# A Mamba-2 and latent-attention inference step on one core: a new step table for the scan's seven steady groups and the output projection

## The chip, the core and the metric

The kernel runs on one core of a Trainium2 chip. The metric is device time in microseconds, the median of several executions. The core has TensorE (PE in the profile; its weight loads are PEld), VectorE (DVE), ScalarE (ACT), GpSimd (POOL) and SyncE (SP, which here only issues DMAs), each with a queue of its own that it works through in order.

## What is computed

Layer 0 is a Mamba-2 state-space layer, layer 1 a latent attention; both see a prompt of 1024 rows and 8 samples of 8 rows, 1088 rows in all, with D = 1024. What the change touches is layer 0 from the input projection to the output projection, cut here to its core:

```python
def ssd_mixer(h, conv_buf, ssm_state, w_in, conv_w, conv_b, dt_bias, a_log, d_skip, norm_w, w_out):
    proj = jnp.einsum('btd,de->bte', h, w_in)
    z, xbc, dt_raw = ...                       # 2048, 2048 + 2*8*128, 32 columns
    xbc, new_buf = causal_conv(xbc, conv_buf, conv_w, conv_b)
    xbc = jax.nn.silu(xbc.astype(F32))         # xs: 32 heads x 64; bm, cm: 8 groups x 128
    y, new_state = ssd_scan(xs, dt, a_head, bm, cm, ssm_state.astype(F32))
    y = y + d_skip.astype(F32)[:, None] * xs
    y = y.reshape(b, t, SSD_D_INNER) * jax.nn.silu(z.astype(F32))
    yg = y.reshape(b, t, SSD_GROUPS, SSD_D_INNER // SSD_GROUPS)
    yg = yg * lax.rsqrt(jnp.mean(yg * yg, axis=-1, keepdims=True) + NORM_EPS)
    out = jnp.einsum('bte,ed->btd', yg.reshape(b, t, SSD_D_INNER) * norm_w, w_out)
```

In ssd_scan a chunk of 128 rows needs, for each of a group's four heads, the decay matrix exp(segment sums) masked to its lower triangle and multiplied with C B^T, that product times x*dt, and a state that goes from chunk to chunk.

## The kernel before

All matmuls work on split numbers: a float32 operand is kept as a high part (a cast to fp32r, on ACT, L129) and a low part (the difference, on DVE or POOL, L130), and a product is three matmuls, high by high, high by low and low by high. So "part p is split" means a cast and a subtraction behind it, of 512 columns of weights, from a raw buffer that a DMA filled ("wraw", two buffers) into "wih" and "wil" (five buffers each). A raw buffer is free for the next load when the low half is done.

The layer runs over 8 groups of heads. ssd_groups treats groups 1 to 7 in the same way, in 21 steps each (t = 0 to 20). In a step of group g TensorE computes one 24-matmul piece of g's input projection (Flow.proj): for t below 12 a block of 128 columns (x, B and C channels, four blocks) for one of three groups of tokens, from t = 12 on the z gate. The other engines meanwhile do the convolution of g (Flow.ew) and the scan of the group before (Scan.ew, Scan.pe), which has 8 chunks of the prompt and a ninth, of 64 rows, for the samples. Behind group 7 a loop of the same form goes through the last scan and through the output projection: OutProj "a" takes the first eight 128-row blocks of w_out, OutProj "b" the other eight, each 18 pieces, one a step, started at steps A0 = 9 and B0 = 27. Its PSUM results are poa and pob. WOut brings w_out's blocks, 512 KB each, and splits them with norm_w (hi on ACT L1053, lo on DVE L1054).

The order of each engine's queue is the order of the program's text (a manual schedule): one step is `ev = fl.proj(t)`, `scan.ew(t)`, `fl.ew(t)`, `ev()` (the eviction of the piece's PSUM on ACT, L571 to L586), `scan.pe(t)`, `fl.pe(t)`. What an instruction waits for is set by tiles and their buffers. PSUM has two banks "tr" (transposes, among them trp, ctp and s0p), two "pj" (projection), and one each for cb, y, pv and st.

Chunk i of the scan: front(i) at step 2i-2 transposes x and B into trp and computes cb = C B^T; front1(i) at step 2i-1 (for i = 0 at step 0) reads these from PSUM: xsT (ACT L699), xdt (DVE L701), BTh and BTl, xdd (POOL), cbm = cb times the mask (DVE L708), and takes four Relu on M (ACT L710). M is the chunk's matrix of summed logarithms, loaded from DRAM by SP (L672, 256 KB), issued a step or two before. front2(i) at step 2i takes Exp of M (L719) and multiplies it with cbm (L723); decayed splits xdd into xddh and xddl, state updates S (L757), out1 and out2 make y. front(i+1) writes the one cb bank, so it waits for cbm of chunk i. From t = 12 on the samples' states come in four parts: turn_state transposes a part into s0p (L826), split_state makes sh and sl of it, state_rows multiplies (pv, L847), add_state and stores follow. copies, turn_copies, triples and blocks prepare the sample rows (b3, xf, x3, bb) for that, in two halves.

In Flow.ew there stand also: the splits of the weights, two per block one step apart (and load(p+2) behind each), parts 10 and 11 both at t = 11; the Silu of the convolved channels at t = 16 and 17 (L626, L627), that of z at 18; the copy "co" of the last three rows of each sequence's channels out of PSUM (ctp, L631) at t = 14 and their six DMAs at t = 15. OutProj scales y by a group's 1/rms, yrs: a pow on POOL over [128, 9x4] (L204, rstd_of), once for a and once for b.

## Time and profile before

| what | us |
|---|---|
| median of 3 runs | 2189.02 |
| lowest and highest run | 2186.99, 2199.06 |
| the profiled execution | 2191.87 |
| its span, first to last instruction | 2190.1 |
| groups 2 to 7, each (five of the windows) | 112.6 to 112.8 |
| output stage before its projection / from poa's first to pob's first matmul | 50.5 / 135.1 |
| the core's mean granted TensorE clock | 0.941 |

Times in the profile's rows are microseconds from the span's start. A window gives the busy time of each engine in a stretch; in the list of waits, a row names the engine and line that waited, the engine and line it waited for, and the total, the number of times and the longest. A timeline row has start, duration, engine, line, operation, output<-input, and in brackets the idle time before it with what ended it.

### The profile page before, as it was taken

How to read it: one execution, taken by the hardware profiler on the slowest of the kernel's cores; microseconds unless marked ns; L12 is line 12 of the kernel's file. 1: busy time of each engine (PE TensorE's matmuls, PEld its weight loads, DVE VectorE, ACT ScalarE, POOL GpSimd, SP SyncE). 2: the span in 40 equal slices, each digit the busy share in tenths (PEclk: the TensorE clock that was granted, in tenths of full speed). 3: DMA queues.
4: the chain of work that ended last, by engine and by line, in shares of the span. 5: the costliest groups of instructions: out<-in, count | busy, mean ns of one | idle time of the engine just before them, and what ended most of it. 6: DMA issues, size and time to landing. Idle time of an engine off the chain costs nothing.

```text
span 2190.1 us, 33508 instructions
## 1 busy us (share of the span) xinstructions
PE 1983.4 (91%) x12001; PEld 1805.7 (82%) x12001; DVE 1245.8 (57%) x2558; ACT 1089.8 (50%) x2547; POOL 809.8 (37%) x977
## 2 busy tenths in 40 slices
PE   6969999999998989858999899979999999989998
PEld 5968988888898989747788799868888887768887
DVE  4427474646465655555443522446787878776665
ACT  5345555555555556553211422433676766655553
POOL 1226364546464646463200001201333333665551
PEclk9979999999899989859999999989999989989999
DMA  4012232323232222244554433132111111364541
GB/s 138 19 54 85 71 88 69 91 59 89 72 85 76 83 73 78 77 146 133 156 179 154 160 140 99 49 99 100 42 43 43 41 41 45 107 211 145 147 135 50
DMA packets 186478, 206.55 MB, mean 94 GB/s; under 512 B 23132, under 2 KB 151912, under 8 KB 185928
## 3 DMA queue, kind: packets, MB, share of 16 engines
q1 hardware_dynamic: 181480, 185.40, 28.1%
q0 software_dynamic: 4752, 18.88, 2.7%
q8 instruction: 95, 1.56, 0.3%
q14 instruction: 71, 0.58, 0.1%
q10 hardware_dynamic: 80, 0.13, 0.0%
HBM read 151.05 MB, written 53.28 MB: 93 GB/s over the span
## 4 chain that ended last, share of the span: by engine, by line
PE 57%; DVE 17%; ACT 8%; issue 7%; DMA 5%; POOL 4%; SPq 1%; POOLq 0%; ACTq 0%; DVEq 0%
PE pj L88 16%; PE pq L100 5%; PE pj L100 5%; PE poa L100 5%; PE pob L100 4%; PE py L734 2%; DVE acc L617 1%; DVE tl L1632 1%; PE pk L100 1%; PE pz L100 1%; POOL kvl L1913 1%; DVE sc L1591 1%; DVE wil L130 1%; PE p L100 1%; PE vp L88 1%
## 5 line engine op out<-in xcount | busy, mean ns | idle before, releaser
L88 PE MATMUL pj<-xh,wih 128*128 128x384 f32 (+1 forms) x768 | 255.8, 337 | 18.0 <-ACT wih L129 9.3
L88 PE MATMUL pj<-xh,wil 128*128 128x384 f32 (+1 forms) x768 | 254.5, 332 | 2.7 <-DVE wil L130 2.0
L88 PE MATMUL pj<-xl,wih 128*128 128x384 f32 (+1 forms) x768 | 254.7, 332 | 0.0
L100 PE MATMUL pj<-wih,xh 128*128 128x256 f32 x504 | 158.9, 319 | 13.5 <-ACT wih L129 13.5
L100 PE MATMUL pj<-wil,xh 128*128 128x256 f32 (+1 forms) x504 | 155.1, 314 | 11.8 <-DVE wil L130 11.8
L88 PEld LDWEIGHTS pj<-xh,wih 128*128 128x128 f32 x768 | 145.9, 191 | 20.0 <-ACT wih L129 9.6
L617 DVE SCALAR_TENSOR_TENSOR acc<-raw,vec,acc 128x1112 f32<-128x1112 f32 x84 | 134.8, 1605 | 40.0 <-ACT acc L613 40.0
L1632 POOL TENSOR_TENSOR tl<-P,th 128x384 fp32r<-128x384 f32 (+1 forms) x96 | 89.6, 933 | 181.9 <-ACT P L1630 137.4
L88 PEld LDWEIGHTS pj<-xh,wil 128*128 128x128 f32 x768 | 146.0, 190 | 7.4 <-DVE wil L130 7.4
L88 PEld LDWEIGHTS pj<-xl,wih 128*128 128x128 f32 x768 | 146.4, 191 | 0.3
L100 PE MATMUL pj<-wih,xl 128*128 128x256 f32 x448 | 139.7, 312 | 0.0
L1629 ACT ACTIVATE th<-st 128x512 fp32r<-128x512 f32 x192 | 94.4, 492 | 74.8 <-PE st L1625 56.2
L100 PEld LDWEIGHTS pj<-wih,xh 128*128 128x128 f32 x504 | 110.8, 220 | 14.9 <-ACT wih L129 14.9
L100 PEld LDWEIGHTS pj<-wil,xh 128*128 128x128 f32 (+1 forms) x504 | 107.8, 214 | 15.3 <-DVE wil L130 14.7
L771 POOL TENSOR_TENSOR y<-y,xD 128x256 f32<-128x256 f32 x64 | 82.1, 1284 | 102.5 <-DVE y L770 102.2
L723 DVE TENSOR_TENSOR M<-M,cbm 128x512 f32<-128x512 f32 (+1 forms) x72 | 54.3, 755 | 91.7 <-ACT M L719 91.7
L1913 POOL TENSOR_TENSOR kvl<-pgr,kvh 128x1024 fp32r<-128x1024 f32 x32 | 78.2, 2445 | 73.4 <-ACT kvh L1912 73.4
L100 PEld LDWEIGHTS pj<-wih,xl 128*128 128x128 f32 x448 | 100.2, 224 | 0.0
L130 POOL TENSOR_TENSOR xddl<-xdd,xddh 128x256 fp32r<-128x256 f32 x64 | 69.2, 1081 | 83.3 <-ACT xddh L129 82.6
L130 DVE TENSOR_TENSOR wil<-wraw,wih 128x512 fp32r<-128x512 f32 x88 | 65.0, 740 | 58.4 <-ACT wih L129 57.5
L710 ACT ACTIVATE M<-M,tok 128x128 f32<-128x128 f32 (+1 forms) x288 | 90.5, 388 | 12.6 <-DMA M<-acs_d 12.5
L1630 ACT ACTIVATE P<-st 128x512 f32<-128x512 f32 x192 | 93.4, 486 | 0.0
(1001 smaller groups left out, 6393.1 us busy)
## 6 DMA issues: line engine op xcount, KB each, us to landing
wraw<-in_ssd_w_in SPq DMA_DIRECT2D x92, 256.0 KB
M<-acs_d SPq DMA_DIRECT2D x64, 256.0 KB
y_d<-xD SPq DMA_DIRECT2D x64, 128.0 KB
s<-in_state_ssm SPq DMA_DIRECT2D x32, 256.0 KB
out_s_ssm<-s SPq DMA_DIRECT2D x32, 256.0 KB
wraw<-in_ssd_w_out SPq DMA_DIRECT2D x16, 512.0 KB
q_d<-qt SPq DMA_DIRECT2D x32, 192.0 KB
qp<-q_d SPq DMA_DIRECT2D x8, 768.0 KB
```

The lines of the kernel that those rows point to most:

```text
L88: nc.tensor.matmul(out, a, b, start=(i == 0), stop=(i == n - 1))
L100: nc.tensor.matmul(o, a, b, start=(j == 0), stop=(j == len(ops) - 1))
L130: (eng or nc.vector).tensor_tensor(lo, src, hi.bitcast(F32), op=ALU.subtract)
L617: nc.vector.scalar_tensor_tensor(acc, raw[:, j : j + n], k.convw[j][:, blk : blk + 1], acc, op0=ALU.mult, op1=ALU.add)
L710: nc.scalar.activation(M[:m, h, :m], M[:m, h, :m], AF.Relu, bias=c.tk[:, 0, 4 * g + h : 4 * g + h + 1], scale=-1.0)
L723: nc.vector.tensor_tensor(M[:m, :, :m], M[:m, :, :m], c.cbm[:m, :m].unsqueeze(1).to_broadcast([m, 4, m]), op=ALU.mult)
L734: nc.tensor.matmul(py[:m, h * 64 : h * 64 + 64], c.M[:m, h, :m], c.xdt[:m, h * 64 : h * 64 + 64], start=True, stop=True)
L771: nc.gpsimd.tensor_tensor(y[:m], y[:m], c.xD[:m], op=ALU.add)
L1629: nc.scalar.activation(th[:, :n], ps[:, :n], AF.Exp, scale=SCALE)
L1630: nc.scalar.activation(P[:, :n], ps[:, :n], AF.Exp, scale=SCALE)
L1632: eng.tensor_tensor(tl[:, :n], P[:, :n], th[:, :n].bitcast(F32), op=ALU.subtract)
L1913: nc.gpsimd.tensor_tensor(rl, raw, rh.bitcast(F32), op=ALU.subtract)
```

## The change

The pieces of the step are put in another order, and some into another step.

- A new method weights_in, called right behind the projection's matmuls and ahead of the scan's work, splits parts 2 to 10 of the weights one step sooner than before, part 11 stays at t = 11 behind the scan's and Flow's work. The next group's part 0 is loaded at t = 10 (was 11) and split at t = 18 (was 19).
- The Silu of x, B, C and of the first z half move into after(t), behind the step's eviction. The copy co moves from t = 14 to 17, its DMAs from 15 to 18, the transposes into ctp from 13 to 16.
- front1 takes the four Relu on M first, then ACT's two PSUM readings (xsT, BTh), then DVE's (xdt, BTl, cbm). front2 comes ahead of decayed; xD goes into a method skip behind out1; add_state goes to the step's end. The second half of the copies moves from t = 14 to 12 and its transposes from 15 to 13; third (b3, xf) is at 11 and 14, triples (bb, x3) at 12 and 16.
- w_out's blocks 0 to 3 are loaded in step 18 of group 7, into four raw buffers; ACT's halves of blocks 0 to 8 are made at steps 0 to 5 ahead of the scan's work, DVE's behind it. Blocks 9 to 15 are loaded from step 21 on through two raw buffers (10 and 11 used to be loaded at steps 9 and 10) and split at steps 21 to 24. A0 becomes 7, B0 25. The pow for a is taken tile by tile ([128, 4]) at t below 9 of group 7, that for b at step 22.

On ScalarE at the start of group 5 (the scan of group 4: xsT4_0 is chunk 0's x, M4_0 its matrix, raw50 the first evicted piece, wih_6577 weights of group 5) stood

```order
L699 COPY xsT4_0_6515<-trp4_0_6474 128x256
L129 CAST BTh4_0_6519<-trp4_0_6474 128x128
L710 ACTIVATE M4_0_6472<-M4_0_6472,tok_71 128x128 x4
L129 CAST xddh4_0_6531<-xdd4_0_6523 128x256
L719 ACT_TABLE_LOAD
L719 ACTIVATE M4_0_6472<-M4_0_6472 128x512
L571 COPY raw50_6481<-pj5_0_6480 128x384
L699 COPY xsT4_1_6572<-trp4_1_6540 128x256
```

and stands now

```order
L700 ACTIVATE M4_0_6472<-M4_0_6472,tok_71 128x128 x4
L702 COPY xsT4_0_6525<-trp4_0_6474 128x256
L705 CAST BTh4_0_6527<-trp4_0_6474 128x128
L722 ACT_TABLE_LOAD
L722 ACTIVATE M4_0_6472<-M4_0_6472 128x512
L129 CAST xddh4_0_6539<-xdd4_0_6533 128x256
L571 COPY raw50_6481<-pj5_0_6480 128x384
L129 CAST wih_6577<-wraw_6468 128x512
```

The four Relu, which read what M's DMA brings, went from behind the two PSUM readings to ahead of them, in chunk 0 as in chunk 1.

On ScalarE in steps 10 and 11 of group 4 (wih is a part of the weights, raw43 an evicted piece, M3_6 the matrix of chunk 6; the first list begins with part 9 and ends with parts 10 and 11, the second begins with part 10 and ends with part 11) stood

```order
L129 CAST wih_5840<-wraw_5702 128x512
L571 COPY raw43_5714<-pj4_10_5794 128x384
L699 COPY xsT3_6_5888<-trp3_6_5849 128x256
L129 CAST BTh3_6_5892<-trp3_6_5849 128x128
L710 ACTIVATE M3_6_5821<-M3_6_5821,tok_71 128x128 x4
L129 CAST Ch3_6_5904<-acc30_4035 128x128
L779 ACTIVATE y3_4_5836,yssq_70<-xD3_4_5691 128x256
L799 CAST b33False_5911<-x3p3False_5855 96x128
L806 CAST x33False_5916<-xf3False_5914 96x256
L129 CAST wih_5919<-wraw_5773 128x512
L129 CAST wih_5926<-wraw_5844 128x512
```

and stands now

```order
L129 CAST wih_5825<-wraw_5689 128x512
L722 ACTIVATE M3_5_5691<-M3_5_5691 128x512
L129 CAST xddh3_5_5837<-xdd3_5_5766 128x256
L129 CAST Sh3_4_5842<-S3_5_5752 128x256
L571 COPY raw43_5720<-pj4_10_5800 128x384
L700 ACTIVATE M3_6_5833<-M3_6_5833,tok_71 128x128 x4
L702 COPY xsT3_6_5898<-trp3_6_5855 128x256
L705 CAST BTh3_6_5900<-trp3_6_5855 128x128
L129 CAST Ch3_6_5910<-acc30_4041 128x128
L786 ACTIVATE y3_4_5846,yssq_70<-xD3_4_5708 128x256
L806 CAST b33False_5917<-x3p3False_5861 96x128
L129 CAST wih_5923<-wraw_5750 128x512
```

Part 10 went to step 10, into the place of part 9 and ahead of chunk 5's Exp; part 11 is where it was, behind the Relu of chunk 6 and what follows them.

On SyncE in steps 10 to 11 of group 4 the queue was

```order
L541 DMA wraw_5773<-in_ssd_w_in 128x2x256
L821 DMA s030_5819<-in_state_ssm 128x4x128
L672 DMA M3_6_5821<-acs_d_1074 128x512
L541 DMA wraw_5844<-in_ssd_w_in 128x2x256
L821 DMA s031_5884<-in_state_ssm 128x4x128
L780 DMA y_d_82<-xD3_4_5691 128x256
```

and is now

```order
L541 DMA wraw_5829<-in_ssd_w_in 128x4x128
L830 DMA s030_5831<-in_state_ssm 128x4x128
L673 DMA M3_6_5833<-acs_d_1074 128x512
L830 DMA s031_5890<-in_state_ssm 128x4x128
L787 DMA y_d_82<-xD3_4_5708 128x256
L541 DMA wraw_5927<-in_ssd_w_in 128x4x128
```

The load ahead of s030 and M3_6 brought part 10 of group 4 (two blocks of 256 columns); now it brings part 0 of group 5 (four of 128), into a raw buffer that part 10 of group 4 has to leave first.

The diff, cut to its core:

```diff
+    def weights_in(self, t):
+        if t < 9 and t % 3 < 2:
+            p = 2 * (t // 3) + 2 + t % 3
+        elif 8 <= t < 11:
+            p = t
+        else:
+            return
+        self.split(p)
+        if p < 10:
+            self.load(p + 2)
+
     def ew(self, t):
         k, g, nc = self.k, self.g, self.k.nc
-        if t < 9 and t % 3:
-            p = 2 * (t // 3) + 1 + t % 3
-            self.split(p)
-            self.load(p + 2)
-        if t in (9, 10):
-            self.split(t - 1)
-            self.load(t + 1)
-        if t == 11:
-            self.split(10)
...
+        if t == 17:
+            self.co = self.rp.tile([128, RAW], F32, tag="raw", name=f"co{g}", bufs=2)[:27, :512]
+            nc.vector.tensor_copy(self.co, self.ctp[:27])
+        if t == 18:
...
+    def after(self, t):
+        nc = self.k.nc
         if t in (16, 17):
             acc, xs = self.xc[t - 16]
             nc.scalar.activation(acc[:, :, :SEQ], acc[:, :, :SEQ], AF.Silu)
             nc.scalar.activation(xs.rearrange("p a (b w) -> p a b w", w=NT),
                                  bass_window(acc, SEQ + 3, NT + 3, NT), AF.Silu)
-        if t == 14:
...
-        if t == 15:
...
         if t == 18:
             nc.scalar.activation(self.z[0], self.z[0], AF.Silu)
-    def late(self, t):
-        if t == 11:
-            self.split(11)
 
     def pe(self, t):
-        if t == 13:
+        if t == 16:
...
         smp = i == 8
+        for h in range(4):
+            nc.scalar.activation(M[:m, h, :m], M[:m, h, :m], AF.Relu, bias=c.tk[:, 0, 4 * g + h : 4 * g + h + 1], scale=-1.0)
         xsT = c.xsT = self.tile([128, 256], "xsT", "xsT" + tag, 1)
         nc.scalar.copy(xsT[:m], p[:m, 0:256])
+        if not smp:
+            c.Bh, c.Bl = (self.tile([128, 128], "BT" + x, "BT" + x + tag, 2, F32R) for x in "hl")
+            nc.scalar.copy(c.Bh, p[:, 256:384])
         xdt = c.xdt = self.tile([128, 256], "xdt", "xdt" + tag, 2)
         nc.vector.tensor_tensor(c.v3(xdt), c.v3(p[:, 0:256]), c.hb(1), op=ALU.mult)
         if not smp:
-            c.Bh, c.Bl = (self.tile([128, 128], "BT" + x, "BT" + x + tag, 2, F32R) for x in "hl")
-            split(k, c.Bh, c.Bl, p[:, 256:384])
+            nc.vector.tensor_tensor(c.Bl, p[:, 256:384], c.Bh.bitcast(F32), op=ALU.subtract)
             c.xdd = self.tile([128, 256], "xdd", "xdd" + tag, 1)
             nc.gpsimd.tensor_tensor(c.v3(c.xdd), c.v3(xsT), c.hb(2), op=ALU.mult)
         cbm = c.cbm = self.tile([128, 128], "cbm", "cbm" + tag, 1)
         nc.vector.tensor_tensor(cbm[:m, :m], c.cb[:m, :m], (k.masks if smp else k.masku)[:m, :m], op=ALU.mult)
-        for h in range(4):
-            nc.scalar.activation(M[:m, h, :m], M[:m, h, :m], AF.Relu, bias=c.tk[:, 0, 4 * g + h : 4 * g + h + 1], scale=-1.0)
...
         nc.scalar.activation(M[:m, :, :m], M[:m, :, :m], AF.Exp, scale=-1.0)
-        c.xD = self.tile([128, 256], "xD", "xD" + c.tag, 2)
-        nc.gpsimd.tensor_tensor(c.v3(c.xD), c.v3(c.xsT), k.dsk[:m, self.hs].unsqueeze(2).to_broadcast([m, 4, 64]),
-                                op=ALU.mult)
         nc.vector.tensor_tensor(M[:m, :, :m], M[:m, :, :m],
                                 c.cbm[:m, :m].unsqueeze(1).to_broadcast([m, 4, m]), op=ALU.mult)
+
+    def skip(self, i):
+        k, c = self.k, self.c[i]
+        m = c.m
+        c.xD = self.tile([128, 256], "xD", "xD" + c.tag, 2)
+        k.nc.gpsimd.tensor_tensor(c.v3(c.xD), c.v3(c.xsT), k.dsk[:m, self.hs].unsqueeze(2).to_broadcast([m, 4, 64]),
+                                  op=ALU.mult)
...
-            if t in (14, 16, 18, 20):
-                self.add_state((t - 14) // 2)
             if i == 0:
                 self.front1(0)
+            if i <= 8:
+                self.front2(i)
             if i < 8:
                 self.decayed(i)
             if 1 <= i <= 8:
                 self.state(i - 1)
-            if i <= 8:
-                self.front2(i)
-            if 1 <= i <= 8:
                 c = self.c[i - 1]
                 self.out1(c, c.py, c.py[:, 256:] if i > 1 else None)
+            if i <= 8:
+                self.skip(i)
+            if t in (14, 16, 18, 20):
+                self.add_state((t - 14) // 2)
         else:
             if t in (13, 15, 17, 19):
                 self.split_state((t - 13) // 2)
...
                 self.front1(i + 1)
             if 1 <= i <= 8:
                 self.out2(self.c[i - 1])
-        if t in (9, 14):
-            self.copies(t == 14)
-        if t in (11, 16):
+        if t in (9, 12):
+            self.copies(t == 12)
+        if t in (11, 14):
+            self.third(t == 14)
+        if t in (12, 16):
             self.triples(t == 16)
-        if t in (12, 16):
-            self.blocks(t == 16)
...
-        if t in (10, 15):
-            self.turn_copies(t == 15)
+        if t in (10, 13):
+            self.turn_copies(t == 13)
...
-        rstd_of(k, self.rs, k.yssq[:, :, k0 // 2 : k0 // 2 + self.ng], 256)
+        self.rs = k.rs
...
-    def split(self, kk, pool=None):
+    def split(self, kk, pool):
         nc, raw = self.k.nc, self.raw.pop(kk)
-        hi, lo = ((pool or self.pool).tile([128, D], F32R, name=f"wo{x}{kk}") for x in "hl")
...
+        nc.scalar.activation(hi, raw, AF.Copy, scale=self.k.ssdn[:, kk : kk + 1])
+        self.late.append((raw, hi, lo, kk))
         return hi, lo
+
+    def low(self):
+        for raw, hi, lo, kk in self.late:
+            self.k.nc.vector.scalar_tensor_tensor(lo, raw, self.k.ssdn[:, kk : kk + 1], hi.bitcast(F32),
+                                                  op0=ALU.mult, op1=ALU.subtract)
+        self.late = []
...
-A0, B0 = 9, 27
+A0, B0 = 7, 25
+
+
+def group_rstd(k, g0, part=None):
+    nc = k.nc
+    if not part:
+        k.rs = k.cs.tile([128, 9, 4], F32, tag="yrs", name=f"yrs{g0}", bufs=1)
+        nc.vector.tensor_scalar(k.rs, k.yssq[:, :, g0 : g0 + 4], 1.0 / 256, EPS, op0=ALU.mult, op1=ALU.add)
+    r = k.rs if part is None else k.rs[:, part]
+    e = k.nhalf[:, : 36 if part is None else 4]
+    nc.gpsimd.tensor_tensor(r, r, e if part is not None else e.rearrange("p (a b) -> p a b", a=9), op=ALU.pow)
...
             ev = fl.proj(t)
+            fl.weights_in(t)
+            if nxt and t == 10:
+                nxt.load(0)
+            if nxt and t == 18:
+                nxt.split(0)
+                nxt.load(2)
             if t == 0 and pscan:
                 gr.ew(21)
                 pscan.ew(21)
             scan.ew(t)
             fl.ew(t)
-            if nxt and t == 11:
-                nxt.load(0)
-            if nxt and t == 19:
-                nxt.split(0)
-                nxt.load(2)
-            fl.late(t)
-            if nxt and t == 11:
-                nxt.load(1)
+            if t == 11:
+                fl.split(11)
+                if nxt:
+                    nxt.load(1)
             if nxt and t == 20:
                 nxt.split(1)
                 nxt.load(3)
+            if t < 9 and not nxt:
+                group_rstd(k, 0, t)
+            if t == 18 and not nxt:
+                als.close()
+                wrs = ExitStack()
+                wo = WOut(k, wrs.enter_context(open_pool(tc, name="wor", bufs=1, side="right")), 4)
+                for kk in range(4):
+                    wo.load(kk)
             ev()
+            fl.after(t)
             scan.pe(t)
             fl.pe(t)
...
-    wo = WOut(k, wa, wa)
-    wo.load(0)
-    wo.load(1)
     wsa, wsb = [], []
-    oa = ob = None
+    oa = OutProj(k, (ya,) * 9, wsa, psum, 0, x_loader(k), "a")
+    ob = None
     for t in range(B0 + 20):
         ev = None
         for o, T in ((oa, A0), (ob, B0)):
...
         if t == 0:
             gr.ew(21)
             pscan.ew(21)
-        if t < 8:
+        if t < 5:
+            for kk in ((0, 1), (2, 3), (4,), (5, 6), (7,))[t]:
+                wsa.append(wo.split(kk, wa))
+        if t == 5:
+            wsb.append(wo.split(8, wx))
+        if t < 22:
             scan.ew(t)
-            wsa.append(wo.split(t))
-            wo.load(t + 2)
-        elif t < 22:
-            scan.ew(t)
-        if t == 4:
-            oa = OutProj(k, (ya,) * 9, wsa, psum, 0, x_loader(k), "a")
-        if t in (9, 10):
-            wsb.append(wo.split(t - 1, wx))
-            wo.load(t + 1)
+        if t < 6:
+            wo.low()
+            for kk in ((4, 5), (6, 7), (8,), (), (), ())[t]:
+                wo.load(kk)
         if t == 21:
+            wrs.close()
...
+            wo = WOut(k, st.enter_context(open_pool(tc, name="wor2", bufs=1, side="right")), 2)
+            wo.load(9)
+            wo.load(10)
+        if t == 22:
+            group_rstd(k, 4)
             ob = OutProj(k, YORD(yb, ya), wsb, psum, NWA, h_loader(k), "b")
-        if 21 <= t < 27:
-            wsb.append(wo.split(t - 11, wb))
-            if t < 25:
-                wo.load(t - 9)
         for o, T in ((oa, A0), (ob, B0)):
             if o:
                 o.ew(t - T)
+        if 21 <= t < 25:
+            for kk in ((9,), (10, 11), (12, 13), (14, 15))[t - 21]:
+                wsb.append(wo.split(kk, wb))
+                wo.low()
+                if kk < 14:
+                    wo.load(kk + 2)
```

More of the change, by code (lines that the diff above doesn't have):

```diff
@@ L912, in ew @@
             c = self.c[8]
-            yo = self.tile([128, 288], "fo", "yo" + c.tag, 1)[:, :256]
+            yo = self.tile([128, 256], "fo", "yo" + c.tag, 1)
             for q in range(2):
@@ L1178, in layer_ssd @@
         k.xl = xp.tile([128, 8, T], F32R, name="xl")
-        al = left.enter_context(open_pool(tc, name="al", bufs=1))
+        als = ExitStack()
+        al = als.enter_context(open_pool(tc, name="al", bufs=1))
         gp = right.enter_context(open_pool(tc, name="gp", bufs=1, side="right"))
@@ L1211, in layer_ssd @@
         with tc.manual_schedule(engines={e.engine for e in (nc.tensor, nc.vector, nc.scalar, nc.gpsimd, nc.sync)}):
-            ssd_groups(k, g0, pools, sp, psum, st, left, right)
+            ssd_groups(k, g0, pools, sp, psum, st, left, right, als)
     stc.close()
```

55 lines of the change are left out of this document (26 added, 29 removed).

## The prediction

> **What bounds the kernel now.** I read the busy shares first, then windows by stage, then what TensorE waits for in one group, then the clock in the stretches behind these waits. The windows view gives core, busy time and instruction count of each engine, granted TensorE clock, share of the DMA engines and GB/s:
>
> ```profile
> 365.50:478.20 112.70, 104.50 (x725) 101.52 (x723) 64.14 (x114) 63.91 (x166) 58.10 (x82) 0.94 0.27 78
> 447.00:450.00 3.00, 1.06 (x9) 0.79 (x8) 2.31 (x4) 0.37 (x1) 2.56 (x5) 1.00 0.00 0
> 450.00:453.40 3.40, 3.40 (x18) 3.40 (x17) 1.48 (x4) 2.33 (x8) 1.62 (x2) 0.50 0.09 33
> 453.40:457.00 3.60, 3.60 (x36) 3.56 (x35) 0.00 (x0) 0.95 (x3) 0.61 (x1) 1.00 0.09 25
> ...
> 467.00:470.50 3.50, 3.50 (x20) 3.39 (x19) 0.41 (x1) 3.37 (x5) 0.00 (x0) 0.51 0.42 129
> ...
> 928.20:978.70 50.50, 23.07 (x93) 18.90 (x91) 28.27 (x51) 29.59 (x70) 33.59 (x32) 0.53 0.47 151
> 978.70:1113.80 135.10, 123.27 (x628) 101.86 (x628) 65.69 (x107) 36.72 (x87) 32.98 (x39) 0.96 0.48 153
> ```
>
> The seven groups are a steady state of about 112.7 us: TensorE busy 104.5, every other engine near half. The next 50.5 us, the start of the output stage, are another regime: TensorE busy 23.07. The stretch behind is filled by TensorE again. In group 4 (478.2 to 591.0) TensorE waits for:
>
> ```profile
> PE pj L100 <- ACT wih L129: 1.9, 1, 1.9
> PE s0p L826 <- DVE co L631: 1.9, 1, 1.9
> PE pj L100 <- DVE wil L130: 1.8, 2, 1.4
> PE pv L847 <- ACT sh L129: 1.7, 1, 1.7
> PE pv L847 <- DVE sl L130: 0.5, 1, 0.5
> PE pj L88 <- DVE wil L130: 0.3, 1, 0.3
> ```
>
> Together 8.1 us, in three places: weights of the first z tile (t=12), the state transposes (t=14), the state products (t=17). The clock shows a second price: from 447 to 450 (t=14 of group 3) TensorE idles for 1.94 of 3.00, from 450.0 to 453.4 it is wholly busy and gets through 18 matmuls, in the next 3.6 us 36. Such a stretch loses half its length, 1.7 us. I find some three a group (the other one shown is at t=17), so the waits cost up to 5 us beyond themselves.
>
> **Part by part, in a group.** (b) *Weights a step sooner.* Parts 10 and 11 of the weights are split in one go before t=12:
>
> ```profile
> 533.20 0.45 SPq L672 DMA_DIRECT2D M<-acs_d  x1
> 535.29 0.61 ACT L129 CAST wih<-wraw 128x512 fp32r<-128x512 f32 x1
> 539.91 1.28 ACT L710 ACTIVATE M<-M,tok 128x128 f32<-128x128 f32 x4
> 543.06 1.13 ACT L129 CAST wih<-wraw 128x512 fp32r<-128x512 f32 x2
> 545.60 1.22 DVE L130 TENSOR_TENSOR wil<-wraw,wih 128x512 fp32r<-128x512 f32 x1
> 546.87 0.58 PE L100 MATMUL pj<-wil,xh 128*128 128x256 f32 x1 [1.44 <-DVE wil L130]
> ```
>
> Part 10 goes to the place of the cast at 535.29, so its waits go: 1.9 on wih and 0.4 of the 1.8 on wil. Part 11 stays at t=11, behind Scan's work, and that work now begins with four Relu that need M of chunk 6. M's load is issued on SP behind a weight load of the next group, which itself waits for the low half of part 10; so I put its issue near 535 (the low half follows a cast like that of 535.29, which now stands earlier in the step), and the Relu, 3.75 behind as at a group's start (below), at 539 to 540. Then come xsT, BTh, Ch, y, b3 and part 11. Now 6.9 us lie between the start of the Relu and the end of the second low half (539.91 to 546.82); without the other part's 0.6 and with xsT and BTh between, some 6.3 to 6.6 remain: part 11 is ready between 545.3 and 546.6, where TensorE now resumes at 546.87. The gain lies between 0 (all of it returns as a wait for part 11) and 3.7 (1.9+1.8). I take 1.7 and, since one idle stretch of half the size need not halve the clock, 1.2 of a possible 1.7 for the clock. Wil's 0.3 of the first steps goes as well (a).
>
> (c) *The co copy behind.*
>
> ```profile
> 561.47 0.67 DVE L631 COPY co<-ctp 27x512 f32<-27x512 f32 x1
> 573.46 1.28 ACT L626 ACT_TABLE_LOAD   x1
> 574.75 1.91 ACT L626 ACTIVATE acc<-acc 128x2048 f32<-128x2048 f32 x1
> 577.17 0.59 ACT L129 CAST sh<-s0p 128x512 fp32r<-128x512 f32 x1
> 577.79 0.69 DVE L130 TENSOR_TENSOR sl<-s0p,sh 128x512 fp32r<-128x512 f32 x1 [2.46 <-ACT sh L129]
> ```
>
> The copy at t=14 frees the "tr" bank that the second s0p needs, 1.9 us late. It goes to t=17, but add_state(0), xf and b3 now stand on VectorE in that step, ahead of the state work; between 0 and 1.9 is won, I take 1.5, and the clock's 1.5 with it. At t=17 the copy (0.67), and at t=18 its six DMAs (at some 0.4 us of issue each on SP, which has no other load there that this step needs), delay nobody as far as I see; if they do, t=17 loses up to 0.67. (d) *Silu behind the eviction.* In step 16 the table load and the Silu, 1.28+1.91, stood ahead of the step's eviction and of sh of t=17, whose readers wait 1.7 for sh and 0.5 for sl. Now they follow the eviction, but sh still queues behind them on ScalarE: what is late next is sh. The step gives about 3.7 us of matmuls as cover (some 37 at the 0.1 us of the window at full clock). Gain between 0 and 2.2; I take 0.8, and 0.6 for the clock.
>
> (e) *Relu ahead of the PSUM readings*, the part that speaks against the change. At the start of group 4:
>
> ```profile
> 479.95 0.46 SPq L672 DMA_DIRECT2D M<-acs_d  x1
> 481.06 0.37 ACT L699 COPY xsT<-trp 128x256 f32<-128x256 f32 x1
> 481.47 0.42 DVE L701 TENSOR_TENSOR xdt<-trp,tok 128x256 f32<-128x256 f32 x1 [0.98 <-ACT xsT L699]
> 481.93 0.27 ACT L129 CAST BTh<-trp 128x128 fp32r<-128x128 f32 x1 [0.49 <-DVE xdt L701]
> 483.70 0.40 ACT L710 ACTIVATE M<-M,tok 128x128 f32<-128x128 f32 x1 [1.51 <-DMA M<-acs_d]
> 482.43 0.28 DVE L708 TENSOR_TENSOR cbm<-cb,masku 128x128 f32<-128x128 f32 x1
> 482.77 0.49 PE L691 MATMUL cb<-acc 128*128 128x128 f32 x2
> ...
>   DMA M<-acs_d: 11.3, 10
> ```
>
> M is used 3.75 us after its issue, with a wait of 1.51 (the last row: 11.3 us in 10 such waits over the groups and the stage's start). It harms nobody, as cbm stands ahead of it and is done at 482.71, just in time for the cb of chunk 1 at 482.77. After the change ScalarE waits for M first, then come four Relu (1.28), xsT (0.37), BTh (0.27), and VectorE's xdt, BTl and cbm behind: cbm ends about 2.66 us after the Relu start. With 483.70 that is 486.4, so cb waits 486.4-482.8 = 3.6; I take 3.5 as the mean over starts, 1.7 for one halved stretch, and 0.2 back for evictions that come sooner: +5.0. Below, it is 0 if M lands before TensorE gets there; above, 3.5 and two halved stretches, +6.7. Queued behind the waiting Relu on ScalarE are also xsT and BTh, and for them POOL's xdd. At the start of group 1 no Relu waits for M in the trace, and I count none.
>
> Front2, add_state to the step's end, xD behind out1 and the bb/x3 split move work among engines that are half idle (64.14, 63.91 and 58.10 of 112.70); I count 0, with what they add at t=14 in (c).
>
> Sum of a group: -0.3 -2.9 -3.0 -1.4 = -7.6; with the start +5.0, -2.6. Six groups -15.6, group 1 -7.6: -23.
>
> **The output stage.** Two of its waits from 928 to 1114, the rows of the weights, and last a window of projection a's matmuls alone (without ScalarE and POOL):
>
> ```profile
> PE ytpa L998 <- issue: 8.6, 2, 4.8
> PE st L88 <- ACT xddh L129: 5.6, 1, 5.6
> ...
> L204 POOL TENSOR_TENSOR yrsa<-yrsa,nhalf x1: 6148/6148/6148, 955.9 to 955.9; 128x36 f32<-128x36 f32 x1
> ...
> 1085.82 0.34 SPq L1047 DMA_DIRECT2D wraw<-in_ssd_w_out  x1
> 1093.55 1.15 ACT L1053 ACTIVATE woh<-wraw,vec 128x1024 fp32r<-128x1024 f32 x1 [2.29 <-DMA wraw<-in_ssd_w_out]
> 1101.01 0.33 SPq L1047 DMA_DIRECT2D wraw<-in_ssd_w_out  x1
> 1105.72 1.15 ACT L1053 ACTIVATE woh<-wraw,vec 128x1024 fp32r<-128x1024 f32 x1 [4.54 <-DMA wraw<-in_ssd_w_out]
> ...
> 1085.00:1113.80 28.80, 26.39 (x115) 19.97 (x113) 4.12 (x6) 1.00 0.72 219
> ```
>
> Projection a starts at step 7, not 9. The nine steps before it last 50.5 us, 5.6 each: two fewer are 11.2. The pow of 6.15 on POOL, behind which xddh waited 5.6, goes into group 7 as nine of four columns. No row shows these: in proportion to columns each is 0.7, 6.1 in all, in POOL's 54 idle us of a group; if each costs the full 6.15, 55.3 fill POOL and group 7 gains up to 10 us. I take the first end: the columns are the same 36. Against 11.2+5.6 stand about 2.5 of moved TensorE work and ytpa waits that stay: I take -14, between -5 and -20. The early loads of w_out (four at t=18 of group 7) stand on SP ahead of the stage's first M; part of that spread.
>
> Projection b loses. Weights 10 and 11 were loaded at t=9 and 10; now 9 to 15 all start at t=21 through two buffers: 9, 11, 13, 15 use one in turn, four round trips. Load to use is 7.7 (1085.82 to 1093.55) or 4.7 (1101.01 to 1105.72), plus 1.15 and some 1.3 for the two halves: 7.1 to 10.1 each, 28 to 40 in all. The cover is steps 21 to 24 of projection a: 24 matmuls a step at 0.23 (26.39 us for 115) are 5.5, four steps 22, some 20 since the last two have the short tile. So b comes 8 to 20 late; I take 9, nearer the quicker of the two loads, though the DMA engines are 0.72 busy there. Stage: -14+9 = -5, between -13 and +14.
>
> **Sum:** -23-5 = -28. The profiled execution took 2191.9 us (span 2190.1): 2164. The median of the three runs is 2.9 lower, 2189.0: 2161.
>
> **Rivals.** *B, the start costs nothing:* M lands before the PSUM readings are due. For it: it waits only 1.51 and in group 1 not at all; against: M's issue keeps its place behind a weight load. Six times 5.0 more: 2131.
>
> *C, slower:* Relu first binds everywhere on M. Each start costs +6.7, part 11 is as late as before (b gains nothing), c and d keep 1.2 and 0.5, with a's 0.3: +4.7 a group, six +28, group 1 -2, and the stage +3 (b's weights later): 2218. It decides from where the Relu at the start hold TensorE over 3 us and M of chunk 6 lands about 4 us behind the low half of part 10. For it: 3.75 us of latency, and cbm with no slack (482.71 against 482.77).
>
> *D, the waits only change places:* part 11, sh and cbm take over what is removed; 2180 to 2200. For it: in b, c and d the next in line is ready within 2 us.
>
> *E, the clock falls only after long idling:* all half clock behind the short waits would then remain, the clock terms of b, c and d (3.3) drop and the start keeps its own: +0.7 a group, 4 in six; group 1 -4.3, stage -5: 2184. Against it: the two waits of 1.9 are the longest of the group, and halved stretches of 3.4 us follow. [...]
>
> **How the numbers follow.** Forecast 0.45, B 0.12, C 0.27, D 0.10, E 0.06. A measurement here tells about 0.5% (11 us) from no change. Faster is forecast and B, less what the stage's upper end takes: 0.55; same is D, E and that rest: 0.18; slower is C: 0.27. The forecast alone spans 2145 to 2178 (stage -13 to +14, b 0 to 3.7); the range must reach B and C, 2122 to 2220.
>
> **What would show it.** Right: groups of 110 us; no wait on co; at group starts cb waiting 3 to 4 us for cbm; poa first some 37 us into the stage instead of 50; pob waiting for the last weights. Wrong: no cbm wait (B), groups of 117 us (C), halved stretches where no wait is left (E), or POOL full in group 7.

## The result: no change that can be measured

In 18 runs each the changed kernel took 2193.74 us in the median (2185.9 to 2203.91), the kernel before 2193.36 (2178.54 to 2203.55): a ratio of 1.0004, interval 0.9985 to 1.0023. The forecast was 2161 from 2189. The profiled execution has a span of 2197.0. By stretches (windows view, first the kernel before, then the changed one; in each the rows are groups 2 to 7, the output stage up to its last matmul, and the attention layer from its first pk matmul on, which the change leaves as it was):

```profile
252.90:928.40 675.50, 625.29 (x4325) 607.52 (x4325) 384.10 (x677) 382.10 (x988) 348.70 (x492) 0.94 0.27 78
928.40:1215.30 286.90, 247.63 (x1196) 204.05 (x1195) 130.35 (x208) 80.51 (x183) 67.47 (x73) 0.90 0.47 150
...
1336.40:2182.60 846.20, 789.54 (x4482) 689.74 (x4480) 577.46 (x1427) 463.76 (x1032) 306.08 (x277) 0.96 0.29 87
```

```profile
247.50:930.80 683.30, 614.76 (x4326) 601.91 (x4325) 390.26 (x677) 378.55 (x988) 338.67 (x501) 0.95 0.27 80
930.80:1211.60 280.80, 245.55 (x1196) 201.19 (x1195) 128.49 (x206) 78.73 (x182) 55.02 (x72) 0.91 0.46 147
...
1332.80:2189.50 856.70, 796.12 (x4481) 695.48 (x4480) 579.90 (x1427) 464.04 (x1032) 305.15 (x277) 0.95 0.29 86
```

Six groups cost 7.8 us more in spite of 10.5 us less TensorE time: the time went into idling, not into the clock. The output stage gained 6.1. Group 1, where nothing waits for M at the start, went from 114.5 to 109.8 us. The attention layer, the same code, differs by 10.5: in the traces of the other kernels below it takes 836 to 852 us, so that much one execution differs from another, and up to its start the changed kernel is 3.6 us ahead. The waits of TensorE in group 5 (592.9 to 705.1) of the changed kernel:

```profile
PE cb L692 <- DVE cbm L713: 4.0, 1, 4.0
PE pj L100 <- DVE wil L130: 2.4, 1, 2.4
PE pj L100 <- ACT wih L129: 1.2, 1, 1.2
PE cb L692 <- DVE s L862: 0.9, 1, 0.9
PE pv L856 <- ACT sh L129: 0.7, 1, 0.7
PE pv L856 <- DVE sl L130: 0.5, 1, 0.5
PE s0p L835 <- issue: 0.4, 1, 0.4
```

The wait for co is gone and that for sh is 1.0 less. Two waits are new: cb's for cbm, the largest (5.0 or 5.1 in the other groups from 2 to 7), and cb's for "s", add_state's sum. The place of the largest, at the start of group 2 (timeline; SyncE, ScalarE, VectorE, TensorE):

```profile
249.69 0.38 SPq L541 DMA_DIRECT2D wraw<-in_ssd_w_in  x1
250.16 0.46 SPq L673 DMA_DIRECT2D M<-acs_d  x1
...
246.51 0.36 ACT L926 COPY yo<-pv 32x256 f32<-32x256 f32 x1 [1.50 <-DMA out_p_ssm<-fo]
...
254.53 1.28 ACT L700 ACTIVATE M<-M,tok 128x128 f32<-128x128 f32 x4 [2.48 <-DMA M<-acs_d]
255.83 0.37 ACT L702 COPY xsT<-trp 128x256 f32<-128x256 f32 x1
...
256.94 0.28 DVE L713 TENSOR_TENSOR cbm<-cb,masku 128x128 f32<-128x128 f32 x1
...
257.28 0.79 PE L692 MATMUL cb<-acc 128*128 128x128 f32 x2 [5.00 <-DVE cbm L713]
```

The order is as forecast: Relu wait 2.48 us for M, 4.37 behind its issue, and cbm ends 2.69 behind their start. But M is issued 2.66 us into the group, not 1.75 as in group 4 before, and yo, ahead of all of it on ScalarE, first waits 1.50 for a store. TensorE's clock then falls to half, as these windows of the same place show (granted clock third from the end):

```profile
251.20:254.60 3.40, 1.08 (x8) 0.81 (x6) 0.31 (x1) 0.58 (x3) 0.00 (x0) 1.00 0.93 243
254.60:261.50 6.90, 4.22 (x14) 4.22 (x15) 2.40 (x6) 6.77 (x18) 2.94 (x4) 0.51 0.26 79
```

For the experiments I cut each group at the first projection matmul of every step. The table has a step's length, then TensorE's idle time in it, in us, as means over groups 2 to 7 of one trace each. By these cuts a group lasts 112.0 to 112.9 us before and 112.2 to 116.5 with the change. The columns e1 to e12 are the experiments below. Of the steps left out, 6 and 9 went from 5.06 and 6.44 to 4.63 and 5.88 with the change, 16 from 3.22 to 3.67, and the rest are alike.

| step | before | changed | e1 | e3 | e5 | e7 | e10 | e12 |
|---|---|---|---|---|---|---|---|---|
| 0 | 4.83/0 | 10.27/4.99 | 6.62/1.49 | 6.02/0.98 | 5.37/0.38 | 5.48/0.48 | 7.39/2.29 | 4.83/0.06 |
| 1 | 5.91/0.24 | 7.27/0 | 6.50/0.63 | 6.55/0.71 | 6.50/0.63 | 6.60/0.72 | 6.22/0 | 5.43/0 |
| 12 | 9.66/3.60 | 8.55/3.48 | 7.40/2.43 | 3.78/0 | 7.38/2.43 | 3.79/0 | 9.35/3.64 | 3.78/0 |
| 13 | 6.80/0 | 6.60/0.14 | 6.11/0 | 8.29/1.75 | 6.39/0 | 8.10/2.06 | 6.83/0 | 8.05/2.06 |
| 14 | 5.98/1.97 | 5.56/1.59 | 5.28/1.31 | 6.58/2.24 | 5.03/1.05 | 5.42/0 | 4.65/0.71 | 4.97/0.17 |
| 15 | 6.91/0 | 5.57/0 | 5.32/0 | 6.06/0 | 5.32/0 | 5.65/0 | 5.31/0 | 5.73/0 |
| 17 | 7.31/2.16 | 6.21/1.20 | 6.20/1.20 | 6.21/1.20 | 6.25/1.20 | 6.45/1.28 | 6.22/1.20 | 6.32/1.31 |
| 18 | 4.64/0 | 3.81/0 | 3.57/0 | 3.56/0 | 3.52/0 | 4.13/0 | 3.80/0 | 3.81/0 |

### The profile page after: what moved, and what is told of

It reads as the page before. It is cut to its first block, busy times and chain, and to the rows that moved or that the text cites. A ratio compares the mean times of both kernels' runs of the same rounds, so it can differ in the third digit from the quotient of the medians.

```text
span 2197.0 us, 33563 instructions
## 1 busy us (share of the span) xinstructions
PE 1973.6 (90%) x12001; PEld 1800.2 (82%) x12001; DVE 1254.4 (57%) x2558; ACT 1085.5 (49%) x2547; POOL 781.3 (36%) x985
## 5 line engine op out<-in xcount | busy, mean ns | idle before, releaser
L100 PE MATMUL pj<-wil,xh 128*128 128x256 f32 (+1 forms) x504 | 145.9, 296 | 16.8 <-DVE wil L130 16.8
L100 PE MATMUL pj<-wih,xh 128*128 128x256 f32 x504 | 149.5, 300 | 8.8 <-ACT wih L129 8.8
L100 PE MATMUL pj<-wih,xl 128*128 128x256 f32 x448 | 131.9, 294 | 0.0
L100 PEld LDWEIGHTS pj<-wil,xh 128*128 128x128 f32 (+1 forms) x504 | 99.0, 197 | 19.1 <-DVE wil L130 18.2
L100 PEld LDWEIGHTS pj<-wih,xh 128*128 128x128 f32 x504 | 102.0, 202 | 10.3 <-ACT wih L129 10.2
L130 DVE TENSOR_TENSOR wil<-wraw,wih 128x512 fp32r<-128x512 f32 x88 | 75.0, 854 | 61.6 <-ACT wih L129 61.3
L778 POOL TENSOR_TENSOR y<-y,xD 128x256 f32<-128x256 f32 x64 | 75.4, 1178 | 85.5 <-DVE y L777 66.3
L707 DVE TENSOR_TENSOR xdt<-trp,tok 128x256 f32<-128x256 f32 (+1 forms) x72 | 30.5, 424 | 118.2 <-ACT BTh L705 116.4
L130 POOL TENSOR_TENSOR xddl<-xdd,xddh 128x256 fp32r<-128x256 f32 x64 | 59.3, 927 | 107.5 <-ACT xddh L129 107.3
L100 PEld LDWEIGHTS pj<-wih,xl 128*128 128x128 f32 x448 | 91.6, 205 | 0.0
```

The source lines that it names most:

```text
L100: nc.tensor.matmul(o, a, b, start=(j == 0), stop=(j == len(ops) - 1))
L130: (eng or nc.vector).tensor_tensor(lo, src, hi.bitcast(F32), op=ALU.subtract)
L707: nc.vector.tensor_tensor(c.v3(xdt), c.v3(p[:, 0:256]), c.hb(1), op=ALU.mult)
L778: nc.gpsimd.tensor_tensor(y[:m], y[:m], c.xD[:m], op=ALU.add)
```

## The experiments

Each was timed in rounds beside the kernel before (medians 2191.65 to 2192.34 there); the ratios are to it, with a 95% interval in brackets.

**e1: Relu behind the PSUM readings again** (front1 of the changed kernel):

```diff
-        for h in range(4):
-            nc.scalar.activation(M[:m, h, :m], M[:m, h, :m], AF.Relu, ...)
         xsT = c.xsT = self.tile([128, 256], "xsT", "xsT" + tag, 1)
...
         nc.vector.tensor_tensor(cbm[:m, :m], c.cb[:m, :m], ...)
+        for h in range(4):
+            nc.scalar.activation(M[:m, h, :m], M[:m, h, :m], AF.Relu, ...)
```

> The changed kernel with one thing undone: the four Relu stand behind the PSUM readings again. Theory: Relu ahead of the readings costs the start of each of groups 2 to 7 some 6.8 us (steps 0 and 1 last 10.3+7.3 us instead of 4.8+5.9) and holds cb 8.9 us at the start of the output stage. Then steps 0 and 1 go back to about 4.8+5.9, groups 2 to 7 become about 107 us long, cb's wait for cbm goes from the group starts, and the time is 40 to 48 us below the changed kernel: a ratio to before of 0.978 to 0.983. Rival (the wait for M only changes its place: Exp and M's product are late, and py waits at step 1): steps 0 and 1 together stay above 14 us, groups stay above 111 us, ratio 0.992 to 1.0.

2144.88 us, ratio 0.9769 (0.9719 to 0.982): the theory, with a little more gain than it gave. Four instructions in another place of one queue cost as much as all the rest of the change brings. A group is 6.8 us shorter in the mean: 4.4 of it in steps 0 and 1, 2.4 in steps 12 to 18. Steps 0 and 1 keep 1.49 and 0.63 of idle time, so they do not come back to what they were before. The wait of 8.9 us that cb has at the start of the output stage was forecast to go with them and did not: it is 8.1 here, and poa begins 41.2 us behind the last projection matmul (changed 41.6). M still comes late, but now behind the readings, where cb no longer waits for it (what it still costs at step 1 is seen in e11); ScalarE at the start of group 7:

```profile
785.19 0.37 ACT L700 COPY xsT<-trp 128x256 f32<-128x256 f32 x1
785.46 0.27 ACT L703 CAST BTh<-trp 128x128 fp32r<-128x128 f32 x1
787.70 1.28 ACT L713 ACTIVATE M<-M,tok 128x128 f32<-128x128 f32 x4 [1.97 <-DMA M<-acs_d]
```

**e4: the kernel before, with Relu first alone:**

```diff
+        for h in range(4):
+            nc.scalar.activation(M[:m, h, :m], M[:m, h, :m], AF.Relu, ...)
         xsT = c.xsT = self.tile([128, 256], "xsT", "xsT" + tag, 1)
...
-        for h in range(4):
-            nc.scalar.activation(M[:m, h, :m], M[:m, h, :m], AF.Relu, ...)
```

> The kernel before with one part of the change alone: the four Relu ahead of the PSUM readings. Theory: this part alone makes the start of a group cost what it costs in the changed kernel: steps 0 and 1 grow by 5 to 7 us in six groups, cb waits 3.6 to 5 us for cbm, ratio 1.013 to 1.020. Rival (the late M at a group's start comes from other parts of the change, such as the six conv DMAs moved to t=18 and DVE's second weight part at t=0): cb waits at most 3.6 and steps 0 and 1 grow by under 4 us, ratio 1.004 to 1.011.

2225.41 us, ratio 1.0136 (1.0085 to 1.0188): the theory. Steps 0 and 1 take 8.87 and 7.57 us, 5.7 more than before, with 3.72 us of idle time. That is the order alone, and nearly the size that the prediction had (5.0, of it 3.5 idle). What the changed kernel has beyond it, 1.3 us of idle time, is from elsewhere in the change.

**e9 and e5: the six conv DMAs at t=20**, in the changed kernel and in e1:

```diff
-        if t == 18:
+        if t == 20:
             sc = k.O["s_conv"].rearrange("o b w c -> (o b w) c")
```

> The changed kernel with the six conv DMAs alone moved from t=18 to 20. Theory: in the changed kernel, too, they make M and the rest of a group's start later, which is the difference between the 5.0 us that cb waits there and the 3.7 it waits when Relu alone is moved in the kernel before: the wait falls to 3.4 to 4.0, step 0 from 10.3 to about 9, 7 to 9 us in all, ratio 0.996 to 0.997. Rival (the M load is what is late, whatever stands ahead of out_p_ssm): the wait stays at 4.8 to 5.1, ratio 0.999 to 1.001.

> The changed kernel with Relu at the back (as in e1_relu_back) and the six conv DMAs at t=20 instead of 18. Theory: at t=18 these six stand on SyncE ahead of out_p_ssm; its end frees the tile that yo needs, so yo, the weight part behind it, M's load and cbm come 1 to 2 us later at each group's start. Then out_p_ssm is issued 2 us sooner, the 1.4 us wait of cb for cbm goes, steps 0 and 1 go from 6.6+6.5 to about 5+6: 1.5 to 2 us in six groups, 9 to 13 us below e1_relu_back, ratio 0.971 to 0.973. Rival (yo is held by add_state, which moved to the end of step 20, or cbm by the two weight parts at t=0): steps 0 and 1 stay within 0.5 us of e1_relu_back, ratio 0.975 to 0.979.

e9: 2180.2 us, ratio 0.9953 (0.9929 to 0.9977); the idle time at the start falls from 4.99 to 4.12 only, so the theory's direction holds, with a little less than its size in the start itself. e5: 2132.53 us, 0.9728 (0.9701 to 0.9755), the theory: step 0 goes from 6.62 to 5.37, though step 1 stays as it was. SyncE at the end of group 4 in the changed kernel shows the queue they made (the first and the last of the six DMAs, and what stands behind them):

```profile
585.38 0.37 SPq L632 DMA_DIRECT2D out_p_conv<-co  x1
...
587.15 0.30 SPq L633 DMA_DIRECT2D out_s_conv<-co  x1
587.55 0.39 SPq L882 DMA_DIRECT2D out_s_ssm<-s  x1
588.04 0.45 SPq L920 DMA_DIRECT2D out_p_ssm<-fo  x1
```

Before, out_p_ssm was issued 8.9 us ahead of the next group's start (582.06 for 591.0), here 4.9 and in group 6 of e1 2.6. fo and yo share one buffer, so yo waits for this store.

**e10: chunk 0's M issued sooner**, Relu still first. The fourth load of the next group's weights moves behind scan.ew(-1):

```diff
                 nxt.split(1)
-                nxt.load(3)
...
         scan.ew(-1)
+        if nxt:
+            nxt.load(3)
         scan.pe(-1)
```

> The changed kernel with chunk 0's M load issued ahead of the next group's fourth weight load (which waits for a low half), so some 5 us sooner; Relu stay first. Theory: the wait at a group's start has two parts, M's landing (2.5 us of ScalarE's idle time) and the four Relu (1.28) ahead of the readings. With M early the first goes and the second stays: cb waits 2.3 to 3 us instead of 5.0, steps 0 and 1 fall by 2.5 to 4 us, 15 to 24 us in all, ratio 0.989 to 0.993, and not as good as Relu at the back (0.977). Rival (the order alone is at fault and M is not late): cb waits 4.5 or more, ratio 0.998 to 1.001.

2160.62 us, ratio 0.9865 (0.9839 to 0.9892), idle time 2.29 instead of 4.99: the theory, with a little more gain than it gave. So the 5.0 us are 2.7 of M's landing and 2.3 of work ahead of cbm.

**e2 and e3: part 11 ahead of the scan's work**, in the changed kernel and in e1:

```diff
-        elif 8 <= t < 11:
+        elif 8 <= t < 12:
...
-            if t == 11:
-                fl.split(11)
-                if nxt:
-                    nxt.load(1)
+            if t == 11 and nxt:
+                nxt.load(1)
```

> The changed kernel with part 11 of the weights split ahead of the scan's work at t=11 too. Theory: the waits of step 12 (1.2 for wih, 2.4 for wil) are part 11 behind the four Relu and what follows them; they go, with most of a half-clock stretch: step 12 from 8.55 us to about 5, 3 to 4 us a group in seven groups, so 20 to 28 us, ratio 0.987 to 0.991; group starts unchanged at 10.3. Rival (part 11's load is late, or the wait goes to the step's other work, such as the M of chunk 6 or the eviction): step 12 stays above 7.5 us or steps 11, 13 and 14 grow by as much; ratio 0.996 to 1.001.

> Both edits. Theory: they are independent: the sum of what each gives, 60 to 76 us below the changed kernel, ratio to before 0.966 to 0.973. Rival (Relu at the back already frees part 11 in time, or the gains share one half-clock stretch): no more than 8 us better than the better of the two.

e2: 2185.78 us, 0.9961 (0.9936 to 0.9986); e3: 2142.93, 0.9757 (0.9707 to 0.9807), 2 us below e1, which is no difference beyond the spread of the runs. By the numbers both went as the rival said: step 12 does what the theory expected (8.55 to 4.31 in e2, 3.78 in e3), but steps 13 and 14 take back 3.1 of the 4.2 us in e2 and 3.5 of 3.6 in e3. The next waits in line, from e2's group 3 and from e3's group 4:

```profile
PE x3p2True L800 <- POOL xr2True L794: 1.8, 1, 1.8
...
541.16 0.68 DVE L862 TENSOR_TENSOR s<-s,sn 128x512 f32<-128x512 f32 x1
...
541.89 0.33 PE L692 MATMUL cb<-xs 128*64 128x64 f32 x2 [2.40 <-DVE s L862]
```

Both are the change's own: the copies for x3p went from t=14 to 12, behind xD on POOL; and add_state went to the step's end, where sn, which it reads, keeps the one cb bank (sn and cb are both taken with the tag "cb") from chunk 8's cb. In e1, where the wait for wih is gone, step 12 keeps its 2.4 us wait for wil: that one is not M's doing; Flow's convolution stands ahead of part 11 on VectorE (the last row is TensorE):

```profile
526.36 1.38 DVE L619 SCALAR_TENSOR_TENSOR acc<-raw,vec,acc 128x1112 f32<-128x1112 f32 x1
527.65 1.23 DVE L130 TENSOR_TENSOR wil<-wraw,wih 128x512 fp32r<-128x512 f32 x1
...
528.93 0.38 PE L100 MATMUL pj<-wil,xh 128*128 128x256 f32 x1 [2.40 <-DVE wil L130]
```

**e6: e3 with add_state in front; e7: besides, conv DMAs at t=20 and the second copies at t=14 to 16:**

```diff
+            if t in (14, 16, 18, 20):
+                self.add_state((t - 14) // 2)
             if i == 0:
                 self.front1(0)
...
-            if t in (14, 16, 18, 20):
-                self.add_state((t - 14) // 2)
```

> The kernel of e3_both with add_state back at the front of the even steps. Theory: sn, which add_state reads, lies in the one bank of cb, so cb of chunk 8 waits at t=14 for add_state at the step's end (2.2 us idle, step 14 is 6.6 us). With add_state in front that goes: steps 14 and 15 from 12.6 to about 10 us, 2 to 3 us in seven groups, 14 to 20 us below e3_both, ratio 0.967 to 0.970. Rival (the 1.7 us wait of x3p for POOL's copies in step 13 already delays what cb waits for): steps 14 and 15 stay above 12 us, ratio 0.974 to 0.978.

> Relu at the back, part 11 early, add_state in front, conv DMAs at t=20, and the second half of the copies and their transposes back at t=14 and 15. Theory: every new wait of the change has a cause of its own among these five, and step 13 falls from 8.3 to about 5.5 us with the copies back: groups of 98 to 102 us, ratio 0.952 to 0.962. Rival (the waits are one chain and only move, into s0p at t=14 and pv at t=17): groups stay above 104 us, ratio 0.967 or more.

e6: 2142.76 us, 0.9776 (0.9747 to 0.9806), no better than e3: by its numbers the rival. In group 4 cb's wait for s shrinks from 2.4 us to 0.3, and s0p waits 2.3 in its place, for the eviction of z. e7: 2123.77 us, 0.9706 (0.9668 to 0.9744), with groups of 104 to 106 us: the rival by both of its numbers, though not in every wait. Step 14 has no idle time any more, but step 13 keeps its 2.06: in group 4 1.3 for sl and sh and 0.8 for cbm.

**e11 and e12: e7 with M early as in e10; and the part of step 0 split behind the scan's work as well:**

```diff
-            fl.weights_in(t)
+            if t:
+                fl.weights_in(t)
...
             fl.ew(t)
+            if not t:
+                fl.weights_in(t)
```

> The kernel of e7_all_back with chunk 0's M load early as in e10_m0_early. Theory: with Relu at the back nothing that TensorE waits for at a group's start depends on M, so it changes nothing beyond 0.3 us a group: ratio 0.968 to 0.973. Rival (Exp and the products of step 1 still wait for M): step 1 falls from 6.6 to under 6 us, 4 to 6 us in all, ratio 0.966 to 0.969.

> The kernel of e11_all_m0 with the weight part of step 0 split behind the scan's work, as before the change. Theory: at t=0 two weight parts stand ahead of the last readings of the group before and of cbm, and that is the 0.5 us idle of step 0 that is left and part of step 1's 0.7: steps 0 and 1 fall from 5.5+6.6 to about 4.9+6.1, 4 to 7 us in all, ratio 0.966 to 0.969. Rival (the part is then late for step 3, or step 1 waits for POOL alone): no change, or a new wait for wil in step 3.

e11: 2117.59 us, 0.969 (0.9644 to 0.9736): by the time either could be right, but step 1 went from 6.60 to 5.43, which is the rival. Since front2 stands ahead of decayed now, xddh is behind Exp on ScalarE, and so behind M, and the state's product waits 0.6 us for its low half xddl (in e7's group 4; in e11 this wait is gone). e12: 2113.86 us, 0.9656 (0.9626 to 0.9686), the lowest median of this study, 78 us below before. Step 0 went from 5.45 in e11 to 4.83, as the theory said; step 1 was at 5.43 in e11 already. The runs of e11 (2110.16 to 2130.52) and of e12 (2110.33 to 2117.66) overlap, so this last gain is seen in the steps and not in the time. What TensorE still waits for in one of e12's groups (448.2 to 552.8):

```profile
PE pv L856 <- DVE sl L130: 1.5, 2, 1.0
PE pv L856 <- ACT sh L129: 1.1, 2, 0.8
PE sn L858 <- DVE cbm L711: 0.8, 1, 0.8
PE cb L692 <- DVE cbm L711: 0.4, 1, 0.4
```

**e8: the projection's starts back at steps 9 and 27** (b's pow at step 24):

```diff
-A0, B0 = 7, 25
+A0, B0 = 9, 27
...
-        if t == 22:
+        if t == 24:
             group_rstd(k, 4)
```

> The changed kernel with the projection's starts back at steps 9 and 27 (the pow of b with them, at step 24). Theory: the two steps sooner are what brought the output stage its gain: poa's first matmul comes 8 to 11 us later than in the changed kernel, while b, which then has two more steps for its seven weight loads, loses none of its 3.5 us to waits; the stage is 5 to 8 us longer, ratio to before 1.002 to 1.004. Rival (the stage's start is bound by the scan's chain and by cb's wait of 8.9, so that the two steps hardly matter): poa first within 3 us of the changed kernel after its bound work, the stage within 2 us, ratio 0.998 to 1.001.

2193.2 us, ratio 1.002 (0.9997 to 1.0043): by the time this cannot be told from the changed kernel (2193.74), so what follows is read from one trace of each. Counted from the last matmul of group 7's projection, poa begins at 48.5 us (before 50.4, changed 41.6), pob at 182.0 (185.6; 175.9), and the stage ends at 284.8 (287.0; 280.9). So in these traces the two steps bring 6.9 us at poa and 3.9 at the end, a little less than expected. What else makes the stage's 6.1 (the early loads, the pow) was not taken apart.

## Why the prediction was wrong, step by step

**The step that failed is the sum of a group, and in it first the term (e), then (b) and (c).** The sum was -2.6 a group, -15.6 in six. The table of steps has, from before to changed: start +6.8 (steps 0 and 1), weights of the first blocks -1.0 (steps 6 and 9), z's first tile -1.3 (12 and 13), co -1.8 (14 and 15), Silu -1.5 (16 to 18): +1.3 a group, +7.8 in six. Of the 23.4 us between, the start makes 11 (+6.8 for +5.0), (b) 10 (-1.3 for -2.9), (c) 7 (-1.8 for -3.0); (a) gives 4 back (-1.0 for -0.3). In (b) and (c) it is the idle time that did not go, while the rest, which the prediction had as the clock's part, came about as put.

**(e)** The mechanism was right: e1 and e4 show it in both directions. Its size was the upper end, +6.7, not +5.0. cb waits 5.0 us instead of 3.5: at group 2, M is issued 0.9 later in the group than in the row that the prediction used and is taken 0.6 later behind its issue (4.37 for 3.75). Two things were counted at nothing: the conv DMAs, of which the prediction said that SyncE had no other load there that the step needs (it has the store out_p_ssm, whose buffer yo needs: e9, e5), and the weight part of step 0 ahead of the last group's remains (e12 shows it with Relu at the back, no run with Relu first). The wait is followed by 6.9 us at a clock of 0.51, in which TensorE is busy for 4.22. An estimate from the prediction's windows (18 matmuls in a busy 3.40 us at 0.50, 36 in 3.60 at 1.00) is that these would take about half of that at full clock, so some 2.1 us are lost and not the 1.7 of one such stretch.

Group 1, without M's wait at its start, gave -4.7 of the -7.6. **(b)** It was taken at -2.9 between 0 and -5.4, and gave -1.3, with no less idle time in steps 12 and 13 (3.62 for 3.60). Part 10 came in time, as argued. Part 11 did not: in group 4 its low half ended 6.3 us behind step 12's start (552.6 for 546.3) where it had ended 6.6 behind (546.8 for 540.2). M of chunk 6, put at an issue near 535, came out at 541.24 in a group that begins 1.8 sooner: the low half that its load waits for stood behind a convolution. That is the smaller part of it: in e1, where part 11 does not stand behind a wait for M, its low half still ends 4.8 behind step 12's start (528.88 for 524.1), behind the convolution; with part 11 ahead of both (e3) step 12 has no idle time.

**(c)** The co copy's wait went as argued (it is not in group 5's list any more), but add_state's move to the step's end, counted at 0, made another at the same place: step 14's idle time fell by 0.4 us, not by 1.5. **(d)** -1.4 was forecast, -1.5 came: sh is still late by 0.7, as written.

**The stage** was right in its sum, -6.1 for -5, but by luck, as both terms were wrong: the first half gained 9.7 up to pob instead of 14, and b lost 3.6, not 9. In the first half xddh's wait behind the pow fell from 5.6 us to 0.6, but cb's longest wait for cbm rose from 3.7 to 8.9. ScalarE waits for no M there; two halves of w_out's blocks (2.17 us) now stand ahead of the readings, but what that wait costs was not tried. In b the seven loads through two buffers were hidden: no wait for a weight is in the list of b's waits, only one of 1.7 at ytpb and one of 1.5 of pob for xra.

**The rivals.** C had the start right (+6.7) and the rest too bad; the outcome lies between the forecast and C, where D was put, though not for D's reason alone: the change does a lot, in both directions. E is out: half clock did hang on waits of under 2 us. In the kernel before, the clock was 0.50 from 450.0 to 453.4, behind a wait of 1.94 us, and step 15, which has no idle time of its own, went from 6.91 to 5.32 in e1, where step 14 idles for 1.31 instead of 1.97. B is out: M was late at the start of each of groups 2 to 7.

## What to carry to other kernels

Put an instruction that waits for a DMA behind what frees a PSUM bank on its queue; here, moving it ahead alone cost 5.7 us at each of six group starts (e4), and moving it back gave 49 us (e1), as much as the rest of a large and useful change brought. Before a DMA issue is moved, look for the stores behind which a buffer comes free on the same queue, and before a reader is moved, for the bank's other tenants. Moved work is worth timing piece by piece: the whole change gave nothing, and two of its pieces undone, the Relu and the conv DMAs, gave 60 us (e5).

## What the runs showed of the hardware that was not expected

The length of a wait alone does not tell here whether the clock is halved behind it. The clock records of the two traces, of the kernel before and of the changed one, have 30 halved stretches in groups 2 to 7 (17 and 13), all at 0.50: 17 last 3.41 us and 13 last 6.83, and within each trace their starts lie whole multiples of 3.413 us apart. I divided both traces at these multiples and took the share of each piece in which TensorE was busy. Behind the 23 full-clock pieces that were busy for 0.43 of their time or less a halved one came each time; of the 20 between 0.45 and 0.65 it came behind 7; behind the 311 from 0.68 up it never came. Of the 43 halved pieces, the 13 that were busy for 0.14 to 0.80 were followed by another halved one, and the 30 that were busy throughout by full clock. That is a count over one execution of each kernel and no more; what decides between 0.45 and 0.65 it leaves open.

In group 7 of the changed kernel, waits of 0.51 and 2.40 us, the longer one across the border of two pieces at 889.5, left the clock at 1.00; these two were busy for 0.63 and 0.52. Behind waits of 0.75 and 0.45 us inside the piece from 916.8 to 920.2, busy for 0.65, the clock was halved from 920.2 on; why it was there and not behind the longer waits, these traces do not show (windows; granted clock third from the end):

```profile
887.40:889.10 1.70, 0.83 (x5) 0.43 (x4) 1.23 (x3) 1.70 (x9) 0.00 (x0) 1.00 0.34 92
889.10:890.80 1.70, 0.00 (x0) 0.00 (x0) 1.70 (x2) 0.65 (x2) 0.72 (x1) 1.00 0.92 277
890.80:892.50 1.70, 1.35 (x11) 1.35 (x12) 1.67 (x6) 0.06 (x1) 0.00 (x0) 1.00 0.06 17
892.50:895.90 3.40, 3.40 (x31) 3.40 (x30) 2.85 (x5) 3.40 (x9) 2.98 (x3) 1.00 0.02 5
...
916.30:918.00 1.70, 0.95 (x8) 0.73 (x6) 0.17 (x1) 1.47 (x3) 0.00 (x0) 1.00 0.00 0
918.00:919.70 1.70, 1.25 (x14) 0.88 (x14) 1.57 (x4) 0.81 (x4) 0.00 (x0) 1.00 0.00 0
919.70:923.10 3.40, 3.40 (x23) 3.33 (x21) 0.56 (x1) 2.34 (x3) 0.00 (x0) 0.58 0.30 83
```

Why the attention layer, the same code, took 836 to 857 us in one execution or another was not tried.
